# Prompt attention scores: the low part of the keys meets the high part of the queries alone, one kv head in each half of the array's rows

## The chip, the cores and the metric

The kernel runs on one core of one Trainium2 chip. The time is that of one launch in microseconds (us), the median of several executions, and lower is better. Engines are named as in the profile: PE multiplies matrices, PEld is its loading of the stationary operand, DVE, ACT and POOL work on vectors, SP issues the DMAs.

## What is computed

One step of a layer with two groups of heads: sliding-window attention (window 128) and an SSM, both fed by one projection `w_in` and gathered by `w_out`. The change touches only the scores of the prompt (512 tokens in four blocks of 128; each block of queries sees its own block of keys and the one before, the first its own alone):

```python
def sink_attend(q, k, v, mask, sink):
    s = jnp.einsum('...qkgd,...skd->...kgqs', q, k).astype(jnp.float32) * (HEAD_DIM ** -0.5)
    s = jnp.where(mask, s, -jnp.inf)
    ...
    return jnp.einsum('...kgqs,...skd->...qkgd', p.astype(v.dtype), v)
```

HEAD_DIM is 64; there are 32 query heads over 4 kv heads.

## The kernel before

Every large product is made in PE's faster float format from operands split into a high part (the value rounded to that format) and a low part (the rest). For the projections three matmuls stand for one, high by high, high by low, low by high (`mm3`, L348 to L350, 288 columns each); they fill nearly the whole run. ACT rounds each piece of weight (L329), DVE takes the rest (L332), four buffers ahead of PE.

The program is written by one recorder: the dense stream of projection matmuls ticks a clock, and side tasks (Python generators) put their instructions between the ticks when their turn and their buffers have come. So each engine gets one fixed order, and PE's is the dense stream with small groups from the side tasks in it. Working tiles (`slots`, `smalls`) are taken from one free list; a task whose tile isn't free comes later.

Attention is done in two passes (`st.pr` 0 and 1), each with two kv heads (`hf` 0 and 1, on partitions 0 to 63 and 64 to 127) and eight pairs of query heads (`jj`). `k_task` prepares the keys of a pass, `q_task` the queries of a pair, and `qb_task` runs twice for a pair (`m`, two blocks of queries each). A pair's query tile `qA` holds the 64 high rows of its first head in rows 0 to 63 and the 64 low rows in rows 64 to 127; `qB` holds those of the second head the other way around. `kHH` holds the high part of the keys twice, one copy under the other, and `kLL` the low part twice. A matmul of `qA` against `kHH` therefore adds up over 128 rows and gives (high + low of the queries) by (high of the keys); one of `qA` against `kLL` adds (high + low) by (low). For each block of queries `qb_task` issues four matmuls, two for each head into that head's bank, and then goes on to the softmax (ACT copy at L975, transposes at L1005, products with the values at L1027). The tokens of the decode batch have a task of their own in each pass (`smp_task`, L1092 to L1147), in two groups of four; its products at L1138 and L1139 alternate between 128 and 8 rows.

Of the kernel before, what the change touches and what calls it, by code (L numbers as in the profile page):

```python
# [9 lines left out]
F32 = mybir.dt.float32  # L10
F32R = mybir.dt.float32r
AF = mybir.ActivationFunctionType
ALU = mybir.AluOpType
# [5 lines left out]
TP = 512  # L19
# [153 lines left out]
def wait(cond):  # L173
    while not cond():
        yield 1
# [3 lines left out]
def kern(ctx: ExitStack, tc: tile.TileContext, a: dict, o: dict):  # L179
    nc = tc.nc  # L180
    V, S, G, PE = nc.vector, nc.scalar, nc.gpsimd, nc.tensor
# [58 lines left out]
    smalls = Small(sch, [])  # L240
# [628 lines left out]
    def k_task(st):  # L869
        kn = st.kn  # L870
        yield from wait(lambda: len(groups[3].done) == 5)
        st.kHH, st.kLL = [], []
        for hf in range(2):
            st.kHH.append((yield from smalls.get(r=True)))
            st.kLL.append((yield from smalls.get(r=True)))
        st.qs = yield from smalls.get()
        st.sgs = yield from smalls.get()
        for hf in range(2):
            src = kn[64 * hf:64 * hf + 64, :TP]
            S.copy(st.kHH[hf][0:64], src)  # L880
            S.copy(st.kHH[hf][64:128], src)
        yield 3
        for hf in range(2):
            r0 = slice(64 * hf, 64 * hf + 64)
            for d0 in (0, 64):
                V.tensor_tensor(st.kLL[hf][d0:d0 + 64], kn[r0, :TP], st.kHH[hf][r0].bitcast(F32), ALU.subtract)
        dma(o["kp"][:, st.pr], kn[:, TP - P:TP])
        dma(o["ks"][st.pr, :, :, 0:120], a["ckT"][st.pr, :, :, 8:P])
        dma(o["ks"][st.pr, :, :, 120:P], kn[:, TP:T].rearrange("p (b t) -> p b t", b=8))
        yield 10  # L890
        st.kready = True
# [47 lines left out]
    def qb_task(st, jj, m, u):  # L939

        j = 8 * st.pr + jj
        yield from wait(lambda: st.kready and st.vready and jj in st.q)
        qA, qB = st.q[jj]
        if u.po is None and not u.asked:
            u.asked = True
            u.po = yield from banks.get()
        yield from wait(lambda: u.po is not None)
        sc = yield from banks.many(2)
        for q in range(2):
            qb = 2 * m + q  # L950
            n = 256 if qb else 128
            keys = slice(128 * (qb + 1) - n, 128 * (qb + 1))
            qc = slice(128 * qb, 128 * qb + 128)
            outs = [sc[hf][:, 256 * q + 256 - n:256 * q + 256] for hf in range(2)]
            for hf, qt in ((0, qA), (1, qB)):
                PE.matmul(outs[hf], qt[:, qc], st.kHH[hf][:, keys], start=True, stop=False)  # L956
                PE.matmul(outs[hf], qt[:, qc], st.kLL[hf][:, keys], start=False, stop=True)  # L957
        u.nq += 1
        if u.nq == 2:
            smalls.put(qA, qB)  # L960
            st.nq += 1
            if st.nq == 8:
                smalls.put(*st.kHH, *st.kLL)
        yield 1

        pslot = yield from smalls.get()
        p4 = pslot[:, :512].rearrange("p (e k) -> p e k", e=4)
        p_ = pslot[:, :512].rearrange("p (f q k) -> p f q k", f=2, q=2)
        t1 = yield from tiny.get()
        t2 = yield from tiny.get()  # L970
        mx, nm, den, es = t1[:, 0:4], t1[:, 4:8], t2[:, 0:4], t2[:, 4:8]
        scv = [t.rearrange("p (q w k) -> p q w k", q=2, w=2) for t in sc]
        f = 0 if m else 1
        for hf in range(2):
            S.copy(p_[:, hf, f:], scv[hf][:, f:, 1])  # L975
        yield 3
        for hf in range(2):
            if f:
                V.tensor_tensor(p_[:, hf, 0], scv[hf][:, 0, 1], mask1, ALU.add)
            V.copy_predicated(p_[:, hf, f:], later.unsqueeze(1).broadcast_to([P, 2 - f, P]), scv[hf][:, f:, 0])  # L980
        banks.put(*sc)
        yield 2
        V.tensor_reduce(mx, p4, mybir.AxisListType.X, ALU.max)
        for src, dst, op in ((nsinkb, nm, None), (nsinkb, es, ALU.subtract)):
            sv = src[:, 2 * j:2 * j + 2].unsqueeze(2).broadcast_to([P, 2, 2])
            dv = dst.rearrange("p (f q) -> p f q", f=2)
            if op is None:
                V.scalar_tensor_tensor(dv, mx.rearrange("p (f q) -> p f q", f=2), -0.125, sv, op0=ALU.mult, op1=ALU.min)  # L988
            else:
                V.tensor_tensor(dv, nm.rearrange("p (f q) -> p f q", f=2), sv, op)  # L990
        yield 4
        for e in range(4):
            S.activation(p4[:, e], p4[:, e], AF.Exp, bias=nm[:, e:e + 1], scale=0.125, accum_out=den[:, e:e + 1])  # L993
        S.activation(es, es, AF.Exp)
        yield 5
        V.tensor_tensor(den, den, es, ALU.add)
        V.reciprocal(den, den)  # L997
        yield 2
        for e in range(4):
            S.activation(p4[:, e], p4[:, e], AF.Copy, scale=den[:, e:e + 1])  # L1000
        tiny.put(t1, t2)
        yield 10
        pt = yield from banks.get()
        for e in range(4):
            PE.transpose(pt[:, P * e:P * e + P], p4[:, e], ident)  # L1005
        yield 1
        pT = yield from smalls.two()
        smalls.put(pslot)
        ptv = pt.rearrange("p (f q k) -> p f q k", f=2, q=2)
        pT4 = [t[:, :512].rearrange("p (f q k) -> p f q k", f=2, q=2) for t in pT]  # L1010

        S.copy(pT[1][:, :512], pt)
        yield 4
        if f:
            V.tensor_tensor(pT4[0][:, :, 1], ptv[:, :, 1], stri.unsqueeze(1).broadcast_to([P, 2, P]), ALU.mult)
        else:
            V.tensor_tensor(pT[0][:, :512].rearrange("p (e k) -> p e k", e=4), pt.rearrange("p (e k) -> p e k", e=4),
                            stri.unsqueeze(1).broadcast_to([P, 4, P]), ALU.mult)
        banks.put(pt)
        yield 8  # L1020
        for q in range(2):
            qb = 2 * m + q
            w0 = 0 if qb else 1
            for w in range(w0, 2):
                for hf in range(2):
                    kc = 128 * qb + 64 * hf
                    PE.matmul(u.po[64 * hf:64 * hf + 64, 128 * qb:128 * qb + 128], (st.vd, st.vt)[w][:, kc:kc + 64], pT4[w][:, hf, q],  # L1027
                              start=w == w0, stop=w == 1)
        smalls.put(*pT)
        u.nv += 1  # L1030
# [526 lines left out]
    for pr in range(2):  # L1557
        st = Pair(pr)
        st.kn, vn = slots.take(), slots.take()
        next_two(("k", pr), ("v", pr), evac_to(st.kn), evac_to(vn), lambda: sch.spawn(k_task(st), 1),  # L1560
                 lambda: sch.spawn(v_task(st, vn), 1), False)
        for jj in range(8):
            j = 8 * pr + jj
            if j == 1:
                drop(*[(kb, 1) for kb in KA])
            qn, gh = slots.take(), slots.take()
            next_two(("q", j), ("g", j), evac_to(qn), evac_to(gh), lambda: None, lambda: None, j == 15 and "all")
            sch.spawn(q_task(st, jj, qn), 1)
            u = Block()
            for m in range(2):  # L1570
                sch.spawn(qb_task(st, jj, m, u), 4 + 26 * m)
            sch.spawn(g_task(st, jj, gh), 3)
            sch.spawn(o_task(st, jj, u), 2)
            if jj == 6:
                sch.spawn(smp_task(st))
# [282 lines left out]
```

## Time and profile before

| what | value |
|---|---|
| time, median of 3 runs | 1605.94 us (1602.54 to 1606.75) |
| time of the profiled execution | 1607.47 us, its span 1605.7 us |
| mean granted clock of PE | 0.99 of full speed |
| busy share of PE, PEld, DVE, ACT, POOL | 98%, 95%, 67%, 48%, 25% |
| matmuls of the scores (L956, L957) | 256 in 32 groups of 8, between 697.9 and 1179.1 us |

The profile gives each instruction a start and a duration. Matmuls overlap in the pipeline, so what one costs PE is read from the distance between two starts, not from its duration. A form such as 64\*128 beside a matmul is the rows and columns of the array that it uses; the figure after it is the shape of its moving operand.

### The profile page before, as it was taken

How to read it: one execution, taken by the hardware profiler on the slowest of the kernel's cores; microseconds unless marked ns; L12 is line 12 of the kernel's file. 1: busy time of each engine (PE TensorE's matmuls, PEld its weight loads, DVE VectorE, ACT ScalarE, POOL GpSimd, SP SyncE). 2: the span in 40 equal slices, each digit the busy share in tenths (PEclk: the TensorE clock that was granted, in tenths of full speed). 3: DMA queues.
4: the chain of work that ended last, by engine and by line, in shares of the span. 5: the costliest groups of instructions: out<-in, count | busy, mean ns of one | idle time of the engine just before them, and what ended most of it. 6: DMA issues, size and time to landing. Idle time of an engine off the chain costs nothing.

```text
span 1605.7 us, 31503 instructions
## 1 busy us (share of the span) xinstructions
PE 1572.0 (98%) x11982; PEld 1524.0 (95%) x11982; DVE 1081.4 (67%) x2067; ACT 771.9 (48%) x1849; POOL 393.6 (25%) x440
## 2 busy tenths in 40 slices
PE   8999999999999999999999999999999999999995
PEld 8999999999999998899999999999989999999995
DVE  7766755774586467588878768778695475655556
ACT  6433434543543346365655645655574333544440
POOL 3201112212322220342223323223102320023323
PEclk9999999999999999999999999999999999999997
DMA  6334356554754648556313332313561286623335
GB/s 245 90 86 104 99 173 192 162 168 147 181 171 158 177 122 269 156 155 142 104 60 110 103 89 73 100 60 93 150 221 51 75 304 197 214 70 91 99 98 192
DMA packets 159783, 222.70 MB, mean 139 GB/s; under 512 B 32424, under 2 KB 68528, under 8 KB 159600
## 3 DMA queue, kind: packets, MB, share of 16 engines
q1 hardware_dynamic: 159632, 220.69, 45.7%
q8 instruction: 94, 1.54, 0.4%
q14 instruction: 57, 0.47, 0.1%
HBM read 181.94 MB, written 40.60 MB: 139 GB/s over the span
## 4 chain that ended last, share of the span: by engine, by line
PE 88%; DVE 4%; ACT 3%; DMA 2%; issue 2%; SPq 1%; POOL 0%; DVEq 0%; ACTq 0%; POOLq 0%
PE bank L348 26%; PE bank L349 25%; PE bank L350 25%; PE bank L1027 2%; PE bank L1338 1%; PE bank L956 1%; PE bank L957 1%; PE bank L1005 1%; PE bank L1350 1%; DVE s L1719 1%; DMA r_d<-t 1%; PE bank L1348 1%; DVE w L332 1%; PE bank L1453 0%; DMA s<-z_d 0%
## 5 line engine op out<-in xcount | busy, mean ns | idle before, releaser
L348 PE MATMUL bank<-x,w 128*128 128x288 f32 x3288 | 992.2, 302 | 2.4 <-ACT w L329 1.3
L350 PE MATMUL bank<-x,w 128*128 128x288 f32 x3288 | 977.6, 297 | 1.7 <-DVE w L332 1.7
L349 PE MATMUL bank<-x,w 128*128 128x288 f32 x3288 | 977.2, 297 | 1.4 <-DVE x L542 1.4
L348 PEld LDWEIGHTS bank<-x,w 128*128 128x128 f32 x3288 | 621.0, 189 | 20.6 <-issue 16.3
L349 PEld LDWEIGHTS bank<-x,w 128*128 128x128 f32 x3288 | 621.2, 189 | 7.1 <-issue 3.8
L350 PEld LDWEIGHTS bank<-x,w 128*128 128x128 f32 x3288 | 621.6, 189 | 2.4 <-DVE w L332 2.4
L332 DVE TENSOR_TENSOR w<-raw,w 128x512 fp32r<-128x512 f32 x476 | 388.4, 818 | 203.4 <-ACT w L329 190.3
L329 ACT CAST w<-raw 128x512 fp32r<-128x512 f32 x476 | 290.4, 616 | 298.6 <-PE bank L349 255.6
L269 POOL TENSOR_TENSOR raw<-raw,raw 128x512 f32<-128x512 f32 x52 | 76.6, 1473 | 193.8 <-issue 166.3
L1217 DVE SCALAR_TENSOR_TENSOR u<-u,c_convwb,u 128x600 f32<-128x600 f32 x72 | 63.8, 886 | 14.3 <-ACT u L1214 13.7
L269 POOL TENSOR_TENSOR raw<-sum,raw 128x512 f32<-128x512 f32 x26 | 33.7, 1294 | 144.3 <-DVE w L332 144.2
L993 ACT ACTIVATE m<-m,t 128x128 f32<-128x128 f32 x128 | 49.9, 391 | 36.7 <-DVE t L988 36.7
L1288 ACT ACTIVATE m<-m,a_tok 128x128 f32<-128x128 f32 (+1 forms) x160 | 53.5, 382 | 22.3 <-DMA m<-aT_d 22.3
L832 POOL TENSOR_TENSOR s<-s,s 128x512 f32<-128x512 f32 (+2 forms) x42 | 45.2, 1076 | 74.3 <-ACT s L830 44.0
L1431 POOL TENSOR_TENSOR m<-m,dch 128x512 f32<-128x512 f32 x32 | 37.6, 1202 | 97.0 <-PE bank L1453 83.9
L1683 POOL TENSOR_TENSOR s<-s,s 128x288 f32<-128x288 f32 x28 | 23.0, 825 | 150.6 <-ACT s L1680 150.6
L542 DVE TENSOR_TENSOR x<-s,x 128x288 fp32r<-128x288 f32 x112 | 48.8, 487 | 15.2 <-ACT x L537 15.0
L830 ACT ACTIVATE s<-s 128x512 f32<-128x512 f32 (+1 forms) x27 | 17.7, 656 | 78.1 <-DVE s L1037 42.9
L1000 ACT ACTIVATE m<-m,t 128x128 f32<-128x128 f32 x128 | 41.0, 392 | 29.4 <-DVE t L997 28.5
L1324 POOL TENSOR_TENSOR m<-m,de 128x512 f32<-128x512 f32 (+1 forms) x20 | 26.6, 1328 | 111.2 <-DVE m L1317 107.6
L269 POOL TENSOR_TENSOR sum<-raw,raw 128x512 f32<-128x512 f32 x26 | 34.4, 1324 | 75.5 <-DMA raw<-in_wout_dram 38.6
L1486 POOL TENSOR_TENSOR s<-s,s 128x576 f32<-128x576 f32 x16 | 25.3, 1581 | 95.2 <-DMA s<-z_d 89.2
(253 smaller groups left out, 1730.6 us busy)
## 6 DMA issues: line engine op xcount, KB each, us to landing
raw<-in_win_dram SPq DMA_DIRECT2D x304, 256.0 KB
raw<-in_wout_dram SPq DMA_DIRECT2D x128, 256.0 KB
s<-m_d SPq DMA_DIRECT2D x80, 288.0 KB
m_d<-s SPq DMA_DIRECT2D x48, 288.0 KB
s<-in_xT_dram SPq DMA_DIRECT2D x40, 288.0 KB
m<-aT_d SPq DMA_DIRECT2D x32, 256.0 KB
m<-in_h0T_dram SPq DMA_DIRECT2D x32, 256.0 KB
out_ss_dram<-m SPq DMA_DIRECT2D x32, 256.0 KB
```

Of the source, the lines that this page charges most:

```text
L269: G.tensor_tensor(dst, x, y, op)
L329: S.copy(w[:, 0], x)
L332: V.tensor_tensor(w[:, 1], x, w[:, 0].bitcast(F32), ALU.subtract)
L348: PE.matmul(out, w[:, 0, c], x[:, 0], start=start, stop=False, skip_group_check=True)
L349: PE.matmul(out, w[:, 0, c], x[:, 1], start=False, stop=False, skip_group_check=True)
L350: PE.matmul(out, w[:, 1, c], x[:, 0], start=False, stop=stop, skip_group_check=True)
L542: V.tensor_tensor(t[:, 1], src, t[:, 0].bitcast(F32), ALU.subtract)
L832: G.tensor_tensor(self.acc[:, c0:c0 + n], self.acc[:, c0:c0 + n], sq[:, :n], ALU.add)
L993: S.activation(p4[:, e], p4[:, e], AF.Exp, bias=nm[:, e:e + 1], scale=0.125, accum_out=den[:, e:e + 1])
L1000: S.activation(p4[:, e], p4[:, e], AF.Copy, scale=den[:, e:e + 1])
L1217: V.scalar_tensor_tensor(y[:, :600], U[:, w:w + 600], cw[:, k, w:w + 1], y[:, :600], op0=ALU.mult, op1=ALU.add)
L1288: S.activation(Mv[q][:n, h, :n], Mv[q][:n, h, :n], AF.Relu, bias=a_tok[:n, c, k:k + 1], scale=-1.0)
```

## The change

The low part of the keys is kept once, in a tile `kL` with the first kv head in rows 0 to 63 and the second in rows 64 to 127. The matmul with it takes only the 64 rows of the query tile that hold the high part, which for `qA` are rows 0 to 63 and for `qB` rows 64 to 127. So the product (low of the queries) by (low of the keys) is no longer computed, and the two matmuls of the two heads use different halves of the array's rows. They now stand next to each other, behind the two matmuls with the high part. `k_task` makes two subtractions in a pass where it made four.

```diff
@@ k_task
-        st.kHH, st.kLL = [], []
+        st.kHH = []
         for hf in range(2):
             st.kHH.append((yield from smalls.get(r=True)))
-            st.kLL.append((yield from smalls.get(r=True)))
+        st.kL = yield from smalls.get(r=True)
...
             r0 = slice(64 * hf, 64 * hf + 64)
-            for d0 in (0, 64):
-                V.tensor_tensor(st.kLL[hf][d0:d0 + 64], kn[r0, :TP], st.kHH[hf][r0].bitcast(F32), ALU.subtract)
+            V.tensor_tensor(st.kL[r0], kn[r0, :TP], st.kHH[hf][r0].bitcast(F32), ALU.subtract)
@@ qb_task
             for hf, qt in ((0, qA), (1, qB)):
                 PE.matmul(outs[hf], qt[:, qc], st.kHH[hf][:, keys], start=True, stop=False)
-                PE.matmul(outs[hf], qt[:, qc], st.kLL[hf][:, keys], start=False, stop=True)
+            for hf, qt in ((0, qA), (1, qB)):
+                r0 = slice(64 * hf, 64 * hf + 64)
+                PE.matmul(outs[hf], qt[r0, qc], st.kL[r0, keys], start=False, stop=True)
         u.nq += 1
         if u.nq == 2:
             smalls.put(qA, qB)
             st.nq += 1
             if st.nq == 8:
-                smalls.put(*st.kHH, *st.kLL)
+                smalls.put(*st.kHH, st.kL)
```

On PE this is the first group of scores. In the rows, `r_7586` and `r_7587` of before (`r_7583` and `r_7584` of now) are the query tiles `qA` and `qB`; `r_7497` and `r_7499` of before are the two high tiles and `r_7498` and `r_7500` the two low ones; now `r_7497` and `r_7498` are the high ones and `r_7499` is `kL`. The last pair of numbers is the shape of the result.

```order
 L350 MATMUL bank_67<-x_543,w_98 128x288
-L956 MATMUL bank_70<-r_7497,r_7586 128x128
-L957 MATMUL bank_70<-r_7498,r_7586 128x128
-L956 MATMUL bank_72<-r_7499,r_7587 128x128
-L957 MATMUL bank_72<-r_7500,r_7587 128x128
...
+L955 MATMUL bank_70<-r_7497,r_7583 128x128
+L955 MATMUL bank_72<-r_7498,r_7584 128x128
+L958 MATMUL bank_70<-r_7499,r_7583 128x128
+L958 MATMUL bank_72<-r_7499,r_7584 128x128
...
 L348 MATMUL bank_67<-x_562,w_98 128x288
```

(The four matmuls of the group's second block of queries, which stand behind each of these fours, are left out.) The number of matmuls is the same, and so is the place of the group in the dense stream; within it the two low ones have moved together. Everywhere from here on, lines behind the change are one higher than before. In the same way all 32 groups change.

On DVE this is the preparation of the keys in the first pass, before:

```order
L1382 SCALAR_TENSOR_TENSOR s_5692<-s_5692,c_dskip,m_6751 128x64
L886 TENSOR_TENSOR r_7498<-s_6964,r_7497 64x512 x2
L886 TENSOR_TENSOR r_7500<-s_6964,r_7499 64x512 x2
L332 TENSOR_TENSOR w_96<-sum_94,w_96 128x512
L906 TENSOR_TENSOR m_7563<-m_7549 128x384
```

and now:

```order
L1383 SCALAR_TENSOR_TENSOR s_5692<-s_5692,c_dskip,m_6751 128x64
L885 TENSOR_TENSOR r_7499<-s_6964,r_7497 64x512
L885 TENSOR_TENSOR r_7499<-s_6964,r_7498 64x512
L332 TENSOR_TENSOR w_96<-sum_94,w_96 128x512
L905 TENSOR_TENSOR m_7560<-m_7546 128x384
```

Two of four subtractions are gone, ahead of a subtraction of weights (L332).

One more thing moves, since one tile less is held: in the first pass the second group of the decode batch (its transposes at L1126, now L1127, its products at L1138 and L1139) comes 24 rows earlier in PE's stream. On PE, before:

```order
L348 MATMUL bank_71<-x_6938,w_96 128x288
L349 MATMUL bank_71<-x_6938,w_96 128x288
L350 MATMUL bank_71<-x_6938,w_96 128x288
L348 MATMUL bank_71<-x_7062,w_96 128x288
L349 MATMUL bank_71<-x_7062,w_96 128x288
```

and now:

```order
L348 MATMUL bank_71<-x_6938,w_96 128x288
L349 MATMUL bank_71<-x_6938,w_96 128x288
L350 MATMUL bank_71<-x_6938,w_96 128x288
L1127 MATMUL bank_68<-ident,m_10326 128x128 x4
L348 MATMUL bank_71<-x_7062,w_96 128x288
L349 MATMUL bank_71<-x_7062,w_96 128x288
```

The instructions of that group are the same ones, and nothing else on PE has another place.

## Rows read from the trace of the kernel before

**Rows 1.** The page: busy times of PE and DVE; the chain that ended last.

```profile
PE 1572.0 (98%) x11982; PEld 1524.0 (95%) x11982; DVE 1081.4 (67%) x2067; ACT 771.9 (48%) x1849; POOL 393.6 (25%) x440
...
PE 88%; DVE 4%; ACT 3%; DMA 2%; issue 2%; SPq 1%; POOL 0%; DVEq 0%; ACTq 0%; POOLq 0%
```

**Rows 2.** Busy times by stretch: the attention stage; PE's granted clock is third from the end.

```profile
690.00:1190.00 500.00, 495.29 (x3903) 481.35 (x3902) 388.93 (x766) 299.00 (x849) 134.50 (x129) 1.00 0.37 108
```

**Rows 3.** PE's waits for others in the same stretch: us, times, longest.

```profile
PE bank L1027 <- DVE m L1017: 1.6, 1, 1.6
PE bank L349 <- DVE x L542: 1.4, 2, 1.2
PE bank L348 <- DVE eT L420: 1.0, 1, 1.0
PE bank L901 <- DVE m L1131: 0.5, 1, 0.5
```

**Rows 4.** The low matmuls (L957) by source line, and their readers.

```profile
L957 PE MATMUL bank<-r,r x128: 272/280/287, 698.0 to 1179.1; 128*128 128x256 f32 x96, 128*128 128x128 f32 x32
...
  ACT m L975: 3.3, 6
```

**Rows 5.** PE in order of time: two groups of scores (start us, us, line).

```profile
697.89 0.22 PE L956 MATMUL bank<-r,r 128*128 128x128 f32 x1
...
698.29 0.34 PE L956 MATMUL bank<-r,r 128*128 128x256 f32 x1
...
698.82 0.29 PE L348 MATMUL bank<-x,w 128*128 128x288 f32 x1
...
704.72 0.28 PE L956 MATMUL bank<-r,r 128*128 128x256 f32 x1
704.84 0.28 PE L957 MATMUL bank<-r,r 128*128 128x256 f32 x1
...
705.66 0.30 PE L348 MATMUL bank<-x,w 128*128 128x288 f32 x1
705.80 0.29 PE L349 MATMUL bank<-x,w 128*128 128x288 f32 x1
```

**Rows 6.** PE in order of time: from 128 rows to 64.

```profile
78.48 0.30 PE L349 MATMUL bank<-x,w 128*128 128x288 f32 x1
78.62 0.29 PE L350 MATMUL bank<-x,w 128*128 128x288 f32 x1
78.84 1.30 PE L741 MATMUL bank<-c_ii,s 64*128 64x32 f32 x10
```

**Rows 7.** PE in order of time: 128 and 8 rows in turn.

```profile
938.18 0.49 PE L1138 MATMUL bank<-m,m 128*128 128x128 f32 x2
938.60 0.48 PE L1139 MATMUL bank<-m,m 8*128 8x128 f32 x2
939.01 0.49 PE L1138 MATMUL bank<-m,m 128*128 128x128 f32 x2
...
940.67 0.40 PE L348 MATMUL bank<-x,w 128*128 128x288 f32 x1
940.91 0.30 PE L349 MATMUL bank<-x,w 128*128 128x288 f32 x1
```

**Rows 8.** PE in order of time: four matmuls of 128 columns, no switch.

```profile
719.44 0.60 PE L1005 MATMUL bank<-ident,m 128*128 128x128 f32 x4
719.79 0.38 PE L348 MATMUL bank<-x,w 128*128 128x288 f32 x1
720.01 0.29 PE L349 MATMUL bank<-x,w 128*128 128x288 f32 x1
```

**Rows 9.** PE in order of time: products in the two halves of the array's columns.

```profile
726.37 1.09 PE L1027 MATMUL bank<-m,m 128*64 128x128 f32 x16
727.39 0.40 PE L348 MATMUL bank<-x,w 128*128 128x288 f32 x1
...
748.30 0.88 PE L1027 MATMUL bank<-m,m 128*64 128x128 f32 x12
749.11 0.40 PE L348 MATMUL bank<-x,w 128*128 128x288 f32 x1
```

**Rows 10.** The subtractions of the keys by source line (ns: min/median/max).

```profile
L886 DVE TENSOR_TENSOR r<-s,r x8: 672/686/1744, 686.7 to 931.1; 64x512 fp32r<-64x512 f32 x8
```

**Rows 11.** Busy times by stretch, around the one fall of PE's clock in this stage.

```profile
690.00:941.30 251.30, 249.63 (x1982) 242.34 (x1981) 199.94 (x392) 152.45 (x430) 75.67 (x71) 1.00 0.38 107
...
941.32:944.73 3.41, 3.41 (x17) 3.41 (x16) 1.23 (x4) 1.30 (x5) 1.31 (x2) 0.50 0.73 179
944.74:948.15 3.41, 3.41 (x28) 3.41 (x27) 2.37 (x4) 1.21 (x2) 1.25 (x1) 1.00 0.18 51
```

## The prediction, made before the changed kernel was run

> **What bounds the kernel now.** I read the busy times and the chain that ended last first [rows 1]: PE is busy 98% of the span and makes up 88% of the chain. A busy share alone can mislead where instructions overlap, so the next view is the stage in question, 690 to 1190 us [rows 2]: PE is busy 495.3 of 500 us there at a granted clock of 1.00 (2.4 GHz), DVE 388.9, ACT 299.0. What PE waits for in this stage is short [rows 3]: 1.6 + 1.4 + 1.0 + 0.5 = 4.5 us. So a microsecond more or less in PE's own stream should come out at the end nearly whole, and one of DVE or ACT hardly at all. Since matmuls are pipelined, the duration of one (281 ns in the median for the low matmuls, [rows 4]) is no price. The distance between starts is: eight matmuls of 256 columns take 705.66 - 704.72 = 0.94 us, 0.1175 each, and four of 128 columns take 698.29 - 697.89 = 0.40 us, 0.10 each [rows 5].
>
> **The change part by part.**
>
> *Two low matmuls side by side.* There are 128 low matmuls, 96 of 256 columns and 32 of 128 [rows 4]. Each pair of them now uses different rows of the array and writes into different banks. No pair in different rows stands in this trace. The nearest rows are the products with the values, which use different halves of the array's columns [rows 9]: a group of 16 reaches the next dense matmul after 727.39 - 726.37 = 1.02 us, one of 12 after 749.11 - 748.30 = 0.81 us. Both contain the same start and end, so four more matmuls cost 0.21 us, 0.05 each, where four that take the whole array cost 0.11 each (next paragraph). Matmuls in different halves do run two at a time. I take the same for halves of the rows, so that one matmul in each pair costs nothing: 48 x 0.1175 + 16 x 0.10 = 7.2 us saved. The two ends are 7.2 us and nothing.
>
> The Trainium skill has this rule for rows as well: "TensorE: Matmul & The Clock Gate", Part 3, Packing small matmuls, lets tiles in different row groups start some 4 ns apart, and puts no price there on going from the whole array to tiles and back. By that page alone the sum would be a gain of 7.2 us; that is the rival on the other side, below. Another page speaks against the change: "TensorEngine Tiling (Array Packing)", Key Properties, says that a change of the tiling mode drains TensorE. It gives no price, so the sum goes by the rows that follow.
>
> *Going into half rows and back.* Before, all eight matmuls of a group use 128 rows, as the dense stream around them does. Now each block of queries goes 128 rows, 128 rows, 64, 64, so each has two switches; 32 groups of two blocks make 128 switches. That a matmul on 64 rows is such a switch is seen where the dense stream meets L741 [rows 6]: from L350 to the first of 64 rows it is 78.84 - 78.62 = 0.22 us, where L349 to L350 is 0.14. So 0.08 us go to emptying the array. After a switch the load of the stationary operand, else hidden, lies open too: from the first dense matmul behind a switch to the second it is 940.91 - 940.67 = 0.24 us [rows 7], 0.10 more than 0.14. The whole price is in the decode products, which alternate between 128 and 8 rows, two matmuls each [rows 7]: 939.01 - 938.18 = 0.83 us hold four matmuls and two switches. Four matmuls of 128 columns without a switch, and one dense matmul behind them, take 720.01 - 719.44 = 0.57 us [rows 8]; less the dense one's 0.14 (705.80 - 705.66, [rows 5]) that is 0.43, or 0.11 each. So two switches cost 0.83 - 4 x 0.11 = 0.39, one 0.195 us, about what the two pieces add up to (0.08 + 0.10). 128 x 0.195 = 25.0 us. The ends: only the emptying is paid, because loads can run ahead into the other half, 128 x 0.08 = 10.2 us; and the full 25.0. I take the full one, since in these rows it is paid in both directions, and it is the row that resembles the new order most. One doubt is kept in the range: those products are in another number format.
>
> *DVE.* Two of four subtractions go in each pass, four in all at 0.69 us [rows 10], 2.7 us of DVE. PE doesn't wait for them: the scores stand after a wait of many ticks on the finished keys, and DVE has 111 us free in this stage [rows 2]. Worth nothing, as a bound 2.7 us.
>
> *Who reads later.* The last low matmul of a group ends some 0.4 to 0.5 us later, and ACT's copy of the scores (L975), which now waits 3.3 us for it in all [rows 4], with it. Behind that copy on ACT stand the rounding of weights for PE; they run up to four buffers ahead, and ACT is idle 201 of 500 us [rows 2]. Hidden; without this cover it would be 32 x 0.5 = 16 us more.
>
> *The decode group that moves* has the same instructions, 24 dense matmuls earlier. It costs what it did, except that its alternation may or may not be followed by a fall of the clock, as one is now at 941.3 us [rows 11]: 17 matmuls stand in 3.41 us at a clock of 0.50 (1.2 GHz), 28 in as much right after at 1.00, so a fall costs 11 x 0.134 = 1.5 us. I take 0, with 1.5 us on each side.
>
> *Sum.* 25.0 - 7.2 = 17.8 us more on PE. DVE's work stays as it is while the stage gets longer, so some of the 4.5 us that PE waits [rows 3] will be gone; I take 1 us off. That makes +16.8 us. The profiled execution took 1607.47 us (span 1605.7) and would take 1624.3; the median of the runs shown lies 1.5 us under it, 1605.94, and so my forecast is 1605.9 + 16.8 = 1622.7, about 1623 us, 1.0% slower.
>
> **The rivals.**
>
> 1. *The pair doesn't run side by side* (the change doesn't do what it says): no credit, +25.0 - 1 = 24, so 1630 us. For it: no two matmuls in different rows are in this trace. Against it: halves of the columns do run in pairs [rows 9].
>
> 2. *It gets faster*: going between the whole array and two halves that fill it together isn't a switch, or is free. Then the 7.2 us are a gain and the time is 1598.7 us. The place is the 128 passages within the groups, and it decides at 7.2 / 128 = 0.056 us for each: below that the kernel gains. Against it: even the emptying alone was 0.08 us at L741, which has 64 rows like the new ones [rows 6], and 0.195 in the alternation [rows 7].
>
> 3. *Only the emptying is paid*, loads being hidden: +10.2 - 7.2 - 1 = +2, so 1608 us, not to be told from no change. Against it: the 0.24 us behind a switch [rows 7].
>
> 4. *The clock falls in these groups.* Before the one fall of this stage [rows 11] PE had alternated between 128 and 8 rows [rows 7]. If each fourth group brought one, 8 x 1.5 = 12 us come on top: 1635 us; with all 32 it would be 48 and 1671. Against it: the value products go from the whole array to its halves and back in each of their groups [rows 9], and the clock stays at 1.00 from 690 to 941.3 us all the same [rows 11].
>
> **How the numbers follow.** The forecast 0.70; rival 1 0.12; rival 2 0.06; rival 3 0.06; rival 4 0.06. A measurement of this kernel tells about 0.3%, 4.8 us, from no change. Slower by more than that are the forecast, rivals 1 and 4: 0.88. Rival 3 is within: 0.06. Rival 2 lies 7 us under and is faster: 0.06. The range reaches up to rival 1 with a fall or so of the clock, 1632 us, and down to where a switch costs half way between its two ends, 0.1375 us (128 x 0.1375 - 7.2 - 1 = +9.4), with two falls of 1.5 us fewer, 1612 us; outside stay rivals 2 and 3 and most of 4.
>
> **What would show each step.** Right: between a group's first matmul and the next dense one some 1.4 us in place of 0.93; the two low matmuls starting within 0.01 us of one another; PEld shown idle ahead of each passage between 128 and 64 rows; the granted clock at 1.00 through this stage as before; DVE and ACT with nothing new to wait for. The first is wrong if groups stay under 0.93 us, the second if the two stand 0.1 us apart. The prediction would be wrong above all if loads for the other half run ahead of the switch, or if the longer groups made PE wait for weights afterwards.

## The result, and the profile after

The changed kernel takes 1619.8 us in the median of 6 runs (1615.64 to 1621.21), the one before 1606.35 us in 6 runs (1602.54 to 1607.14). The ratio is 1.0087, with a 95% interval of 1.0074 to 1.0100: slower by 13.4 us. The forecast was 1623 us, 16.8 us slower; the direction and the range hold, the size is somewhat high. The profiled execution took 1620.12 us, its span 1618.3 us, where before it was 1607.47 and 1605.7.

The page of the changed kernel shows the same picture as [rows 1], and that is the first thing to learn from it:

```profile
PE 1583.5 (98%) x11982; PEld 1521.5 (94%) x11982; DVE 1082.6 (67%) x2063; ACT 774.9 (48%) x1849; POOL 392.8 (24%) x440
...
PE 86%; DMA 4%; DVE 4%; ACT 3%; issue 2%; POOL 1%; SPq 1%; DVEq 0%; ACTq 0%; POOLq 0%
```

PE is as busy as before, at 98%, with as many matmuls. PE has no new wait for another engine; what was added is counted as busy time. It has to be read from the starts. This is PE in order of time in the group that answers to the second one of [rows 5], two blocks of 256 columns (start us, us until the last end, line):

```profile
704.06 0.40 PE L955 MATMUL bank<-r,r 128*128 128x256 f32 x2
704.39 0.38 PE L958 MATMUL bank<-r,r 64*128 64x256 f32 x2
704.70 0.50 PE L955 MATMUL bank<-r,r 128*128 128x256 f32 x2
705.13 0.39 PE L958 MATMUL bank<-r,r 64*128 64x256 f32 x2
705.45 0.40 PE L348 MATMUL bank<-x,w 128*128 128x288 f32 x1
705.69 0.30 PE L349 MATMUL bank<-x,w 128*128 128x288 f32 x1
```

From the first matmul to the next dense one it is 705.45 - 704.06 = 1.39 us, where it was 0.94. The records of the two low matmuls (L958) start 0.003 us apart, in the mean of the 64 pairs, and both are over 0.38 us after the first start, as long as a single one behind a switch takes (L957 in the third experiment below): they run side by side. Yet from each pair to the next matmul on all rows it is 0.31 us (704.39 to 704.70, 705.13 to 705.45). The two high matmuls behind a switch end late (0.50 us for two, against 0.40 for the two ahead of which no switch stands), and the dense matmul behind the group is 0.24 us ahead of its follower, not 0.14.

PEld's list of the stage says what is missing in those places. Columns: busy us, mean ns of one, and behind the last bar its idle time, here with no releaser named. The first two lines are of the kernel before, the last two of the changed one:

```profile
L956 PEld LDWEIGHTS bank<-r,r 128*128 128x128 f32 x128 | 24.2, 189 | 0.0
L957 PEld LDWEIGHTS bank<-r,r 128*128 128x128 f32 x128 | 24.2, 189 | 0.0
...
L955 PEld LDWEIGHTS bank<-r,r 128*128 128x128 f32 x128 | 19.8, 188 | 3.2
...
L958 PEld LDWEIGHTS bank<-r,r 64*128 64x128 f32 x128 | 11.9, 183 | 7.6
```

Before, the loads of both lines had no idle time ahead of them. Now PEld is idle for 7.6 us ahead of the 64 pairs on half rows and for 3.2 us ahead of the loads on whole rows behind them, and ahead of the dense loads (L348) its idle time has gone from 6.9 to 9.9 us. A load also no longer runs ahead of its matmul. In the second group of [rows 5] the load of the first low matmul starts 0.12 us ahead of it (the matmul at 704.84); in the group above the two start together (the matmul at 704.39). PEld before, then now:

```profile
704.72 0.19 PEld L957 LDWEIGHTS bank<-r,r 128*128 128x128 f32 x1
...
704.38 0.19 PEld L958 LDWEIGHTS bank<-r,r 64*128 64x128 f32 x2
```

That the array empties while PEld is idle is the reading of it; no view shows the emptying itself. PE's waits for others have gone down a little, from 4.5 us in [rows 3] to 3.0:

```profile
PE bank L1028 <- DVE m L1018: 1.6, 1, 1.6
PE bank L349 <- DVE x L542: 1.2, 1, 1.2
PE bank L348 <- DVE eT L420: 0.2, 1, 0.2
```

Added up over the 32 groups, from the first matmul of each to the next dense one in the same view, it is 42.5 us now and was 29.9 us: 12.5 us more. Another 0.106 us in each, 3.4 us in all, stands between that dense matmul and the one behind it. That makes 15.9 us more in PE's stream.

How much of it comes through is read between the starts of the first and the last group, with 31 of the 32 groups in between, that is 15.4 of the 15.9 us. The last group of the kernel before, then the first and the last of the changed one:

```profile
1178.29 0.28 PE L956 MATMUL bank<-r,r 128*128 128x256 f32 x1
...
697.07 0.33 PE L955 MATMUL bank<-r,r 128*128 128x128 f32 x2
697.34 0.33 PE L958 MATMUL bank<-r,r 64*128 64x128 f32 x2
697.59 0.50 PE L955 MATMUL bank<-r,r 128*128 128x256 f32 x2
...
1192.16 0.40 PE L955 MATMUL bank<-r,r 128*128 128x256 f32 x2
```

It is 1192.16 - 697.07 = 495.1 us, where it was 1178.29 - 697.89 = 480.4 [rows 5]: 14.7 us more. But in this execution PE's clock fell twice between the two groups, from 946.22 to 949.63 us and from 1181.74 to 1185.15 us, and before only once [rows 11]. At the 1.5 us for a fall that the prediction works out, some 13.2 of the 15.4 us come through, and about 2 us were taken out of PE's waits and other small gaps. The fifth experiment's kernel shows the same without the second fall: the same groups, one fall as before, and 13.5 us.

### The profile page after: what moved, and what is told of

The parts are those of the page before. It is cut to its first block, busy times and chain, and to the rows that moved or that the text cites. A ratio compares the mean times of both kernels' runs of the same rounds, so it can differ in the third digit from the quotient of the medians.

```text
span 1618.3 us, 31498 instructions
## 1 busy us (share of the span) xinstructions
PE 1583.5 (98%) x11982; PEld 1521.5 (94%) x11982; DVE 1082.6 (67%) x2063; ACT 774.9 (48%) x1849; POOL 392.8 (24%) x440
## 4 chain that ended last, share of the span: by engine, by line
PE 86%; DMA 4%; DVE 4%; ACT 3%; issue 2%; POOL 1%; SPq 1%; DVEq 0%; ACTq 0%; POOLq 0%
PE bank L348 25%; PE bank L349 24%; PE bank L350 24%; PE bank L1028 2%; DMA s<-z_d 1%; PE bank L955 1%; PE bank L958 1%; PE bank L1339 1%; PE bank L1006 1%; DVE s L1720 1%; PE bank L1351 1%; DMA z_d<-s 1%; DMA r_d<-t 1%; PE bank L1349 1%; DMA s<-m_d 1%
## 5 line engine op out<-in xcount | busy, mean ns | idle before, releaser
L348 PE MATMUL bank<-x,w 128*128 128x288 f32 x3288 | 994.5, 302 | 1.4 <-ACT w L329 1.2
L348 PEld LDWEIGHTS bank<-x,w 128*128 128x128 f32 x3288 | 619.2, 188 | 23.3 <-issue 16.4
L332 DVE TENSOR_TENSOR w<-raw,w 128x512 fp32r<-128x512 f32 x476 | 389.1, 820 | 202.0 <-ACT w L329 187.1
L542 DVE TENSOR_TENSOR x<-s,x 128x288 fp32r<-128x288 f32 x112 | 49.7, 494 | 16.9 <-ACT x L537 16.6
L1001 ACT ACTIVATE m<-m,t 128x128 f32<-128x128 f32 x128 | 41.2, 397 | 23.2 <-DVE t L998 23.1
```

The lines of the kernel that those rows point to most:

```text
L332: V.tensor_tensor(w[:, 1], x, w[:, 0].bitcast(F32), ALU.subtract)
L348: PE.matmul(out, w[:, 0, c], x[:, 0], start=start, stop=False, skip_group_check=True)
L542: V.tensor_tensor(t[:, 1], src, t[:, 0].bitcast(F32), ALU.subtract)
```

## The experiments

The theory is that of the prediction, with its price taken from the groups just shown: each passage between 128 and 64 rows costs PE about 0.18 us, (15.9 + 7.2) / 128, and a pair in two halves of the rows saves one matmul. The rivals are that the new order costs, that a matmul on half rows is dear in itself, that the pair gains nothing, and that the clock or DVE has a part in it. The first four ran beside one another on one chip, with 1604.25 us for the kernel before (23 runs); the fifth ran later, with 1605.14 us (9 runs).

**The change's product and order, on whole rows.** The low tile of each head is filled up with zeros, so that the product (low by low) is left out as in the change.

```diff
-        st.kL = yield from smalls.get(r=True)
+        st.kL = [(yield from smalls.get(r=True)), (yield from smalls.get(r=True))]
...
+            z0 = slice(64 - 64 * hf, 128 - 64 * hf)
+            V.tensor_tensor(st.kL[hf][z0], st.kHH[hf][z0].bitcast(F32), st.kHH[hf][z0].bitcast(F32), ALU.subtract)
-            V.tensor_tensor(st.kL[r0], kn[r0, :TP], st.kHH[hf][r0].bitcast(F32), ALU.subtract)
+            V.tensor_tensor(st.kL[hf][r0], kn[r0, :TP], st.kHH[hf][r0].bitcast(F32), ALU.subtract)
...
-                r0 = slice(64 * hf, 64 * hf + 64)
-                PE.matmul(outs[hf], qt[r0, qc], st.kL[r0, keys], start=False, stop=True)
+                PE.matmul(outs[hf], qt[:, qc], st.kL[hf][:, keys], start=False, stop=True)
```

> The low part of the keys meets the high part of the queries alone, as in the change, and the two low matmuls stand behind the two high ones, but each uses all 128 rows: the low tile of each head holds zeros in the rows of the queries' low half. No switch between 128 and 64 rows is left, and no pair runs side by side. Theory of switches (each passage between 128 and 64 rows costs PE about 0.18 us, a pair in two halves of the rows saves one matmul): neither cost nor saving, so the time of before, 1606 us within 4, and groups of scores of 0.93 us. Rival, the new order itself (high, high, low, low, and its readers later) is what costs: the time of the changed kernel, 1620 us.

Measured: 1604.71 us, ratio 1.0005 (0.9993 to 1.0017). PE in order of time, L957 being the high and L959 the low matmuls:

```profile
701.89 0.41 PE L957 MATMUL bank<-r,r 128*128 128x256 f32 x2
702.13 0.40 PE L959 MATMUL bank<-r,r 128*128 128x256 f32 x2
702.37 0.40 PE L957 MATMUL bank<-r,r 128*128 128x256 f32 x2
702.61 0.40 PE L959 MATMUL bank<-r,r 128*128 128x256 f32 x2
702.84 0.30 PE L348 MATMUL bank<-x,w 128*128 128x288 f32 x1
```

0.95 us, as before. The order, the later end of the low matmuls and the product left out cost nothing and gain nothing. Zeros in half of the rows take as long as numbers. One part of the change is missing here besides the half rows: as many tiles are held as before, so the second decode group stands in its old place. That group takes as long in either place; in the kernel before and in the changed one:

```profile
937.45 0.39 PE L1138 MATMUL bank<-m,m 128*128 128x128 f32 x2
...
942.80 0.38 PE L1139 MATMUL bank<-m,m 128*128 128x128 f32 x2
...
946.02 0.46 PE L348 MATMUL bank<-x,w 128*128 128x288 f32 x1
```

It is 940.67 - 937.45 = 3.22 us before [rows 7] and 946.02 - 942.80 = 3.22 us now. So the change's time lies in the use of half rows.

**Half as many switches.** All four low matmuls of a group stand behind its four high ones. Both blocks of queries of a head share a bank, and only the first high matmul in it is still issued with `start`.

```diff
             for hf, qt in ((0, qA), (1, qB)):
-                PE.matmul(outs[hf], qt[:, qc], st.kHH[hf][:, keys], start=True, stop=False)
+                PE.matmul(outs[hf], qt[:, qc], st.kHH[hf][:, keys], start=q == 0, stop=False, skip_group_check=True)
+        for q in range(2):
...
             for hf, qt in ((0, qA), (1, qB)):
                 r0 = slice(64 * hf, 64 * hf + 64)
-                PE.matmul(outs[hf], qt[r0, qc], st.kL[r0, keys], start=False, stop=True)
+                PE.matmul(sc[hf][:, 256 * q + 256 - n:256 * q + 256], qt[r0, qc], st.kL[r0, keys], start=False, stop=q == 1, skip_group_check=True)
```

> As in the change, but the four high matmuls of a group (both blocks of queries) come first and its four low ones, on half rows, after them: the same number of half-row matmuls, and two switches in a group in place of four. Theory of switches: 64 x 0.18 = 11.5 us of switches less 7.2 us saved by the pairs, +4.3 us on PE, less about 0.5 absorbed: 1610 us, groups of about 1.08 us. Rival, a matmul on half rows is dear in itself: as the changed kernel, 1620 us and groups of about 1.33 us.

Measured: 1608.61 us, ratio 1.0026 (1.0014 to 1.0039), 4.4 us over before.

```profile
700.28 0.64 PE L955 MATMUL bank<-r,r 128*128 128x256 f32 x4
700.85 0.50 PE L963 MATMUL bank<-r,r 64*128 64x256 f32 x4
701.28 0.40 PE L348 MATMUL bank<-x,w 128*128 128x288 f32 x1
701.52 0.30 PE L349 MATMUL bank<-x,w 128*128 128x288 f32 x1
```

The group takes 1.00 us, and 0.10 more behind it; the expected 1.08 had both. Four low matmuls are over in 0.50 us. With the same 128 half-row matmuls the extra has gone from 13.4 to 4.4 us, which a price of the half-row matmul itself can't do. Over the 32 groups PE has 31.57 - 29.93 + 3.38 = 5.0 us more, so a switch costs (5.0 + 7.2) / 64 = 0.19 us.

**Twice as many switches, and no pairs.** The order of before, high and low of one head and then of the other, with the low ones on half rows.

```diff
             for hf, qt in ((0, qA), (1, qB)):
+                r0 = slice(64 * hf, 64 * hf + 64)
                 PE.matmul(outs[hf], qt[:, qc], st.kHH[hf][:, keys], start=True, stop=False)
-            for hf, qt in ((0, qA), (1, qB)):
-                r0 = slice(64 * hf, 64 * hf + 64)
                 PE.matmul(outs[hf], qt[r0, qc], st.kL[r0, keys], start=False, stop=True)
```

> As in the change, but in the order of before (high and low of the first head, then of the second): four switches in each block of queries, 256 in all, and no two half-row matmuls side by side. Theory of switches: 256 x 0.18 = 46 us with nothing saved, less about 1 us absorbed: 1652 us, groups of about 2.4 us. Rival, the half-row matmul itself is dear: the change's extra without the pairs' saving, 1620 + 7 = 1627 us. If longer stretches of switching let PE's clock fall, the time lies above 1652 us and the granted clock of 690 to 1190 us under 0.98.

Measured: 1649.45 us, ratio 1.0276 (1.0252 to 1.0299), 45.2 us over before.

```profile
703.74 0.28 PE L956 MATMUL bank<-r,r 128*128 128x256 f32 x1
703.94 0.38 PE L957 MATMUL bank<-r,r 64*128 64x256 f32 x1
704.25 0.38 PE L956 MATMUL bank<-r,r 128*128 128x256 f32 x1
704.57 0.38 PE L957 MATMUL bank<-r,r 64*128 64x256 f32 x1
...
705.82 0.38 PE L957 MATMUL bank<-r,r 64*128 64x256 f32 x1
706.13 0.40 PE L348 MATMUL bank<-x,w 128*128 128x288 f32 x1
```

Each matmul but the first is now behind a switch and stands 0.31 us from its follower, where in the group of before they stood 0.1175 apart: 0.19 us for the switch. In its groups PE has 48.1 us more (74.4 - 29.9, and 0.11 behind each), 1.3 of them in one group at half the clock, so a switch costs (48.1 - 1.3) / 256 = 0.18 us; in the medians 45.2 us come out. The clock was at 1.00 up to the decode products, though each group now alternates for 2.4 us, and at 0.99 in the stage. Busy times by stretch (the granted clock is third from the end):

```profile
690.00:959.10 269.10, 269.10 (x1961) 247.85 (x1960) 201.03 (x387) 155.40 (x431) 75.24 (x71) 1.00 0.35 98
...
690.00:1190.00 500.00, 500.00 (x3602) 460.63 (x3600) 360.53 (x686) 274.24 (x756) 131.21 (x126) 0.99 0.31 91
...
1208.45:1222.00 13.55, 12.63 (x45) 11.23 (x46) 10.04 (x24) 7.90 (x23) 1.84 (x2) 0.50 0.53 183
```

The last of them is the one place where a group of scores, the last but one, ran at 1.2 GHz. That fall began ahead of the group, behind two waits of PE for DVE (1.64 and 1.17 us, which the changed kernel has as well: the first two of its list above).

**The same switches, and no pairs.** Both low matmuls take rows 0 to 63.

```diff
             for hf, qt in ((0, qA), (1, qB)):
-                r0 = slice(64 * hf, 64 * hf + 64)
-                PE.matmul(outs[hf], qt[r0, qc], st.kL[r0, keys], start=False, stop=True)
+                PE.matmul(outs[hf], qt[:64, qc], st.kL[:64, keys], start=False, stop=True)
```

> As in the change, but both low matmuls use rows 0 to 63 (the second head's takes the wrong half of its operands, so its low product is not computed). The switches are those of the change, and the two can't run side by side. It measures what the side by side of the pair is worth. If halves of the rows do run two at a time: 64 x 0.11 = 7 us more than the changed kernel, 1627 us, with the two starts about 0.12 us apart. Rival, the pair gains nothing, since each of the two waits for the other's load: as the changed kernel, 1620 us.

Measured: 1626.43 us, ratio 1.0136 (1.0116 to 1.0157).

```profile
701.60 0.40 PE L955 MATMUL bank<-r,r 128*128 128x256 f32 x2
701.93 0.50 PE L957 MATMUL bank<-r,r 64*128 64x256 f32 x2
702.36 0.50 PE L955 MATMUL bank<-r,r 128*128 128x256 f32 x2
702.79 0.50 PE L957 MATMUL bank<-r,r 64*128 64x256 f32 x2
703.22 0.40 PE L348 MATMUL bank<-x,w 128*128 128x288 f32 x1
```

Two low matmuls take 0.50 us, where in two halves they take 0.38 and 0.39. Their starts are 0.22 us apart, not the 0.12 expected, but the next high matmul then follows 0.21 us behind the second in place of 0.31, so that the pair as a whole takes 0.12 us more (0.43 from its start to the next high one, against 0.31). The groups add up to 49.7 us against 42.5: the pairs are worth 7.2 us. The ratios differ by 0.0049, 7.9 us, and their intervals do not overlap (from 1.0116 here, up to 1.0100 for the change). So the change's saving is there in full; it is only smaller than what it costs to reach it.

**The subtractions of before.** The two subtractions of a pass are issued twice.

```diff
-            V.tensor_tensor(st.kL[r0], kn[r0, :TP], st.kHH[hf][r0].bitcast(F32), ALU.subtract)
+            for _ in range(2):
+                V.tensor_tensor(st.kL[r0], kn[r0, :TP], st.kHH[hf][r0].bitcast(F32), ALU.subtract)
```

> The changed kernel, but with each of its two subtractions of a pass issued twice, so that DVE has the four of before again (2.7 us more in all). If they were hidden, as the prediction has it: the ratio of the changed kernel to before again, 1.009, within 0.002. Rival, the change's 2.7 us less of DVE work had paid for a part of the new switches: up to 2.7 us more, a ratio of 1.0105 or over.

Measured: 1619.21 us, ratio 1.0081 (1.0065 to 1.0097), not to be told from the change's 1.0087. The upper end, 1.0097, lies under the rival's 1.0105: the four subtractions were hidden. Its trace also shows what the groups bring through with one fall of the clock in the stage (958.96 to 962.37 us), as before:

```profile
698.99 0.33 PE L956 MATMUL bank<-r,r 128*128 128x128 f32 x2
...
1192.85 0.39 PE L956 MATMUL bank<-r,r 128*128 128x256 f32 x2
```

From the first group to the last it is 493.9 us, 13.5 more than the 480.4 of before, with groups as long as the change's (42.5 us in all).

## Why the prediction was right, and where its size was off

*The bound.* PE's stream sets the end of this stage: of 15.4 us added between the first and the last group, 13 to 13.5 us came through (a second fall of the clock set aside), and of 48.1 us in the interleaved kernel 45.2 in the medians. The 1 us taken off for shorter waits was about 2.

*The pair.* "I take the same for halves of the rows": shown. The saving of 7.2 us was worked out from the distances in [rows 5], and the kernel with both in one half gives it back to the tenth. Rival 1 falls.

*The switch.* Two parts were forecast, the array emptying and then a load with nothing to hide it. PEld's idle time, the loads that start with their matmuls and the distances of 0.31 us bear it out, as far as the views reach. Rival 2, that halves filling the array together are no switch, falls with the groups of 1.39 us, and rival 3, that loads run ahead, with the 0.24 us behind each group. Here lies the largest part of the size that was off: 0.195 us for each made 25.0 us; measured are 0.18 us and 23.1 us in the changed kernel (0.19 with half as many switches, 0.18 with twice as many). The difference lies in the blocks of 128 columns. Worked out in the same way, the groups with two blocks of 256 columns give 0.194 us a switch, those with one of 128 give 0.167 in the mean, which leaves 0.14 for the switches of that block; behind its pair the next high matmul follows after 0.25 us (697.34 to 697.59), not 0.31.

*Where the price came from* was in part luck. The "four matmuls without a switch" of [rows 8] carry an extra of their own: behind them the dense matmul is 720.01 - 719.79 = 0.22 us ahead of its follower, nearly as much as behind a switch in [rows 7], though no form changes there. So 0.24 us behind a product is no sign of a switch by itself; in the changed kernel it is one, since behind the same scores it was 0.14 before. And that extra went into the 0.11 us taken for each matmul. From the first of the four to the dense one it is 719.79 - 719.44 = 0.35 us, 0.09 each, and with that the alternation gives (0.83 - 0.35) / 2 = 0.24 us for a switch and a forecast some 6 us higher. The decode products, with 128 columns, 8 rows and the other number format, are thus dearer to switch than the scores with 128 columns (0.14); which of the two differences does it was not tried. That 0.195 nearly met the scores at 256 columns was not known beforehand.

*The rest of the difference.* The switches are 1.9 of the 3.4 us between the forecast's +16.8 and the measured +13.4, whose interval reaches from 11.9 to 16.1 us. About 1 us more was taken out of PE's waits than was taken off. The half microsecond that is left is less than the interval tells. In the two profiled executions the second fall in the stage is set off by 2.0 us outside it: the first group starts 0.8 us earlier in the changed kernel, and from the last group to the end it takes 1.2 us less. Before the stage, where both programs are the same, the granted clock of one stretch was 0.50 before and 1.00 after. The kernel before:

```profile
94.83:98.22 3.39, 3.39 (x15) 3.39 (x15) 3.39 (x9) 2.49 (x5) 0.70 (x2) 0.50 0.31 67
```

The changed one:

```profile
94.80:98.20 3.40, 3.40 (x30) 3.27 (x28) 2.96 (x8) 2.81 (x6) 0.39 (x2) 1.00 0.15 33
```

The change can't have made this difference; such falls come and go from one execution to the next, and they are a likely part of why the runs of one kernel spread over 4 to 6 us, which was not measured.

*What hides behind what.* The low matmuls end later, and ACT's copy waits for them 17.2 us in all, where it was 3.3 us [rows 4]; nothing on PE waits for it in turn, as predicted:

```profile
  ACT m L976: 17.2, 26
```

So ACT waits longer, which the prediction's part on the readers foresaw and its list of signs left out; it costs nothing. Rival 4 falls: the granted clock of the stage is 0.99, not the 1.00 of before, but no fall of the clock begins in a group of scores, neither here nor with twice the switches. The DVE term was rightly put at nothing.

*A version that beats both* is not among these kernels. The numbers say what it needs: a stay on half rows costs two switches, 0.36 us, and each pair in it saves 0.12, so more than three pairs must stand together. The change has one pair for each stay, the second experiment two. With all four pairs of a query tile in one stay the sum would be 32 x 0.18 - 7.2 = -1.4 us, less than these measurements tell from nothing. That needs four banks for the scores at once, where the kernel takes two; it was not tried on the chip.

## What to carry to other kernels

In this kernel two matmuls on half of the array's rows run at the price of one, but going from whole rows to half rows and back costs PE about 0.36 us, the saving of three pairs of 256 columns. So gather the half-row matmuls until, by these numbers, more than three pairs stand together (not tried here), or fill up with zeros and stay on whole rows, which cost nothing here. None of it is seen in a busy share or a list of waits: read the distance between the starts of two matmuls on either side of the change of form, and the idle time of the loads.

## What the runs showed of the hardware that was not expected

The price of a switch hardly depends on its direction: in the interleaved kernel it is 0.31 us from start to start on the way in and on the way out, 0.19 us over the undisturbed distance. It does depend on the columns: in the blocks of 128 the starts of that kernel are 0.25 us apart, where they were 0.10 before [rows 5], 0.15 us for a switch:

```profile
696.03 0.32 PE L957 MATMUL bank<-r,r 64*128 64x128 f32 x1
696.28 0.33 PE L956 MATMUL bank<-r,r 128*128 128x128 f32 x1
696.54 0.32 PE L957 MATMUL bank<-r,r 64*128 64x128 f32 x1
696.79 0.38 PE L956 MATMUL bank<-r,r 128*128 128x256 f32 x1
```

And PE and PEld keep their busy shares (98%, and 94% after 95%) while 23.1 us go to switches, since the record of a matmul behind a switch starts with its load, not behind it, and is longer: 0.38 us in place of 0.28.

The changed kernel has a fall behind the same two waits of PE as the interleaved one, but it lasts only from 1181.74 to 1185.15 us and ends ahead of the next group of scores. In the interleaved kernel the low clock goes on through that group, for 13.55 us. The kernel before has both waits as well (1.64 us until 1166.24, 1.17 us until 1168.84) and no fall behind them before 1190 us. Whether the alternation held the clock down can't be said from one case:

```profile
1181.74:1185.15 3.41, 3.41 (x16) 3.41 (x15) 3.41 (x7) 1.50 (x4) 1.34 (x1) 0.50 0.35 97
```
